# Background dots kept out of an FFN's first slice, and eight low parts per FFN taken from GpSimd to VectorE

## The chip, the cores and the metric

One core of one Trainium2 chip runs the whole program. The metric is device time in microseconds (us) of one execution. The engines are PE (TensorE matmul), PEld (TensorE's weight loads), DVE (VectorE), ACT (ScalarE), POOL (GpSimd) and SP (SyncE, which here issues the DMAs). L566 is line 566 of the kernel before.

## The reference, cut to what matters

A backbone of two layers. Each layer is an FFN, a token mixing, and a second FFN, so that there are four FFNs, which are called FFN 1 to FFN 4 here in the order of time. Tokens are 512 latent and 256 context columns (three groups of 256 columns, called G_A, G_B and G_C in the kernel, with G_C the context), the width is 1024, and the FFN's inner width is 2816. Everything is float32.

```python
def pre_mod(x, g, m, slot):
    return rmsnorm(x, g) * (1 + m[:, None, 3 * slot + 1]) + m[:, None, 3 * slot]

def post_residual(x, y, g, m, slot, weight):
    return x + weight * m[:, None, 3 * slot + 2] * rmsnorm(y, g)

def ffn_sublayer(x, m, slot, g_pre, g_post, wg, wu, wd):
    h = pre_mod(x, g_pre, m, slot)
    y = (jax.nn.silu(h @ wg) * (h @ wu)) @ wd
    return post_residual(x, y, g_post, m, slot, 0.5)
```

The vectors `m` (shift, scale and gate of each sub-layer) are a product of SiLU(c) with a matrix of 1024 x 9216 per layer. They depend on nothing else, so the kernel computes those of later sub-layers in the background, while matmuls run: these are the "dots" of this text.

## The kernel before, in words

**Products.** Every float32 operand is split into a high part (`whi`, `zh`, a rounded copy made by ACT) and a low part (`wlo`, `zl`, the remainder, a subtraction on DVE or POOL). A product is three matmuls: high by high, high by low, low by high (`mm3`, L519, L520, L522). Weights arrive as 128x1024 float32 tiles in a buffer with the tag "raw" (four of them), are copied by ACT to `whi` (L93) and subtracted to `wlo` (L94), on POOL unless the caller names DVE. `whi` and `wlo` have five buffers each.

**An FFN** (`ffn`) walks over 22 blocks `f` of 128 inner columns, in six slices of 4, 4, 4, 4, 2 and 4 blocks. In slice 0 the blocks 0 and 1, and the gate half of block 2 where there is no `begin`, are done group of tokens by group, since each group's input comes out of a chain of the norms before it (`post` and `prez`: squares on ACT, sums in the tiles `be` on DVE or POOL (L405), a matmul with ones on PE (L155), a power on POOL (L159), a broadcast by PE (L165), and the tiles of z from L469 on DVE). This first part of an FFN is called its head here. Block 2's other half follows, then block 3 and all later ones go through `fast`: seven products of half the width and half the depth, in the manner of Strassen, on sums and differences of the quarters. `combine` (L550 to L579) makes the combined inputs once per FFN, between the head and block 3: for each of four k the four DVE steps L560 to L563 on the tiles `y`, then a copy to `t42h` by ACT and the low part `t42l` on POOL (L566, 128x768; 128x512 in FFN 4, which has no context); at last for each k a copy of a half by ACT (L577) and its low part `t` on POOL (L578, 128x384; 128x256 in FFN 4). `combine_t1` (L581 to L586) adds four more pairs, with DVE. `evac` moves a block's result out of PSUM: SiLU by ACT (L546), the product `sg` on DVE (L547, at high priority), then `gh` on ACT and `gl` on DVE (L539). After each slice `down` multiplies by the down weights in chunks (two blocks of 128 rows of output each for a slice of four), first slice to `y` by ACT (L783), later slices added on DVE.

**Dots.** `ada_bg` (L353 on) puts items on the list `bg`: a load of a 128x1024 tile `abraw` into a "raw" buffer by SP (L237), and one or two dots on DVE (L243, one for each vector: two in the items before FFN 4's, one there). `pump` (L114 to L126) places them: each call adds `rate` to `credit`, with rate the items over 57; where no load is ahead it only issues one load and returns; otherwise it places items while the credit is at least 1, and each item also issues the next item's load. `pump(False)` adds credit alone. `ffn` calls it in block 2 after the gate half and after the evacuation, `fast` calls it twice per block (with `bg`, false for the last block of a slice), `down` once per chunk. The credit is carried from FFN to FFN.

**Order.** Each engine runs its queue in order. The order in a queue is that of a scheduler which plays the program on a simulated timeline: it takes program order as the priority among what is ready there, except for pieces under `high_priority`. So an instruction can stand in its engine's queue far from where the program places it.

The lines that the change touches: L566 and L578 in `combine`; L735 in the loop over a slice's blocks; and the three calls of `pump` in block 2 of slice 0 (L743, L751, L754).

Of the kernel before, what the change touches and what calls it, by code (L numbers as in the profile page):

```python
# [5 lines left out]
F32 = mybir.dt.float32  # L6
# [28 lines left out]
class K:  # L35
# [488 lines left out]
    def ffn(self, l, i, slot, groups, post, begin=None):  # L524

        nc, d = self.nc, self.d
# [5 lines left out]
        def loads(f, eng=None):  # L532
            return [self.load_w(d["wu"][l, i, f, u], eng=eng) for u in range(2)]
# [7 lines left out]
        def evac(j, pg, pu, off, n):  # L541
            for o in range(0, n, 256):
                sg = self.sg()[:, :256]
                c = slice(o, o + 256)
                with self.tc.high_priority():
                    nc.scalar.activation(sg, pg[:, c], AF.Silu)  # L546
                    nc.vector.tensor_tensor(out=sg, in0=pu[:, c], in1=sg, op=ALU.mult)  # L547
                gated(j, sg, off + o, 256)

        def combine():  # L550


            n1, n2, w = slice(0, nh), slice(nh, 2 * nh), 2 * nh
            t42 = [[self.tx(4 * x + k, f"t42{'hl'[x]}", F32R) for x in range(2)] for k in range(4)]
            t3 = [self.tx(8 + k, "t3", F32R) for k in range(4)]
            V = nc.vector
            F = {n: [] for n in ("b11", "b21", "b22", "t1", "t2", "t3", "t4")}
            for k in range(4):
                y0, y4 = self.y[k], self.y[k + 4]
                V.tensor_sub(y0[:, n1], y0[:, n2], y0[:, n1])  # L560
                V.tensor_sub(y0[:, n2], y4[:, n2], y0[:, n2])
                V.tensor_sub(y4[:, n2], y4[:, n2], y0[:, n1])
                V.tensor_sub(y4[:, n1], y4[:, n1], y4[:, n2])  # L563
                h, lo = t42[k]
                nc.scalar.copy(h[:, :w], y4[:, :w])
                nc.gpsimd.tensor_sub(lo[:, :w], y4[:, :w], h[:, :w].bitcast(F32))  # L566
                zh, zl = self.zh[k], self.zl[k]
                F["t3"].append((t3[k][:, :nh], t3[k][:, nh:w]))
                F["t4"].append((h[:, n1], lo[:, n1]))
                F["t2"].append((h[:, n2], lo[:, n2]))  # L570
                F["b11"].append((zh[:, n1], zl[:, n1]))
                F["t1"].append((zh[:, n2], zl[:, n2]))
                for n, c in (("b21", n1), ("b22", n2)):
                    F[n].append((self.zh[k + 4][:, c], self.zl[k + 4][:, c]))
            for k in range(4):
                th, tl = F["t3"][k]
                nc.scalar.copy(th, self.y[k][:, n2])  # L577
                nc.gpsimd.tensor_sub(tl, self.y[k][:, n2], th.bitcast(F32))  # L578
            return F  # L579

        def combine_t1(F):  # L581

            for k in range(4):
                h, lo = F["t1"][k]
                nc.scalar.copy(h, self.y[k][:, :nh])
                nc.vector.tensor_sub(lo, self.y[k][:, :nh], h.bitcast(F32))  # L586
# [69 lines left out]
        for s, nf in enumerate(SLICES):  # L656
            gh = [self.fp.tile([P, NT], F32R, tag=f"gh{j}", name=f"gh{j}") for j in range(nf)]
            gl = [self.fp.tile([P, NT], F32R, tag=f"gl{j}", name=f"gl{j}") for j in range(nf)]
            f0 = SL0[s]
            j0 = 0  # L660
            if s == 0:
                j0 = 2
                todo = groups
                W2 = None
                if begin is None:
                    W = [loads(f, nc.vector if (3 >> f) & 1 else None) for f in range(2)]
                    if 1:

                        W2 = self.load_w(d["wu"][l, i, 2, 0], eng=nc.vector if 0 else None)
                        pl, pc = self.bank(), self.bank() if has_c else None  # L670
                        part = {G_A: pl[:, 0:256], G_B: pl[:, 256:512], G_C: has_c and pc[:, :256]}
                else:

                    todo, W, pb = [G_C], [], {}

                    def part(f, ks):
                        for u in range(2):
                            wh, wl = W[f][u]
                            if (f, u) not in pb:
                                pb[f, u] = self.bank()  # L680
                            for k in ks:
                                self.mm3([(pb[f, u], 0, NL)], wh[:, k * P : (k + 1) * P], wl[:, k * P : (k + 1) * P], k, k == 0, k == KT - 1)

                    next(begin)
                    W.append(loads(0))
                    next(begin)
                    W.append(loads(1))
                    if 1:
                        next(begin)
                        part(0, range(4))  # L690
                        next(begin)
                        part(1, range(4))
                        for f in range(2):
                            part(f, (4, 5))
                    else:
                        part(0, range(4))
                        next(begin)
                        part(0, (4, 5))
                        part(1, range(6))
                        next(begin)  # L700
                    for f in range(2):
                        part(f, (6, 7))
                        evac(f, pb[f, 0], pb[f, 1], 0, NL)
                    next(begin)
                for g in todo:
                    off, n, v = g
                    self.drain(g)
                    for f in range(2):
                        ps = []
                        for u in range(2):  # L710
                            b = self.bank()[:, :n]
                            ps.append(b)
                            wh, wl = W[f][u]
                            for k in range(KT):
                                self.mm3([(b, off, n)], wh[:, k * P : (k + 1) * P], wl[:, k * P : (k + 1) * P], k, k == 0, k == KT - 1)
                                if k in ((3, 7) if 1 else (7,)):
                                    self.step()
                            if not 1:
                                self.step()
                        evac(f, ps[0], ps[1], off, n)  # L720
                    if W2:
                        wh, wl = W2
                        for k in range(KT):
                            self.mm3([(part[g], off, n)], wh[:, k * P : (k + 1) * P], wl[:, k * P : (k + 1) * P], k, k == 0, k == KT - 1)
                            if k == 3:
                                self.step()
                        self.step()
            if s == 0:
                self.drain()
                F = combine()  # L730
            for j in range(j0, nf):
                if f0 + j > 2:
                    if f0 + j == 3:
                        combine_t1(F)
                    fast(f0 + j, j, F, j < nf - 1)  # L735
                    continue
                ps = []
                pre = s == 0 and j == 2 and W2
                W = [None, self.load_w(d["wu"][l, i, 2, 1])] if pre else loads(f0 + j)
                for u in range(2):  # L740
                    if pre and u == 0:
                        ps.append([(pl, 0, NL)] + ([(pc[:, :256], NL, NC)] if has_c else []))
                        self.pump()  # L743
                        continue
                    wh, wl = W[u]
                    outs = [(self.bank()[:, :n], off, n) for off, n in full]
                    for k in range(KT):
                        self.mm3(outs, wh[:, k * P : (k + 1) * P], wl[:, k * P : (k + 1) * P], k, k == 0, k == KT - 1)
                    ps.append(outs)
                    if u == 0:  # L750
                        self.pump()  # L751
                for (pg, off, n), (pu, _, _) in zip(*ps):
                    evac(j, pg, pu, off, n)
                self.pump()  # L754
            self.down(d["wd"][l, i], SL0[s] * 1024, gh, gl, nf, s == 0, s == len(SLICES) - 1, groups, full, post, (l, slot))

    def down(self, wd, base, gh, gl, nf, first, last, groups, full, post, at):
# [1258 lines left out]
```

## Time and profile before

| | us |
|---|---|
| median of three runs | 3329.84 |
| lowest, highest run | 3324.64, 3330.06 |
| the profiled execution | 3321.82 |
| span of its profile | 3320.0 |
| FFN 2, FFN 3, FFN 4 in the span (about) | 1250 to 1790, 1793 to 2340, 2927 to 3320 |

Busy times are the time in which an engine executed instructions, as a share of the span. A wait of an engine is idle time in front of an instruction, put down to the instruction that released it (`PE rb L155 <- POOL be L405` is PE idle in front of a matmul of line 155 into `rb`, until POOL's operation of line 405 on `be` was done). The granted clock of PE is given as a share of its full speed of 2.4 GHz; its mean over this execution was 0.953. DVE steps that share memory with a POOL operation are longer than the same steps elsewhere, and the rows show it.

### The profile page before, as it was taken

The numbers are of one execution on the slowest core, as the hardware profiler recorded it, in microseconds if no ns is written. First come the engines' busy times: TensorE is split into PE (matmuls) and PEld (weight loads), VectorE is DVE, ScalarE is ACT, GpSimd is POOL, SyncE is SP. The second block draws the span as 40 slices with busy tenths as digits, with TensorE's granted clock in tenths as the row PEclk, the third lists the DMA queues.
The fourth block names the chain that finished last, engine by engine and source line by source line (L and its number), as shares of the span: only waits on it lengthen the run. The fifth ranks groups of instructions, "written<-read, shape, count | busy, mean of one in ns | idle before, by whom it ended". The sixth has DMA issues, their size and how long they took to land. (4 is left out here: it accounts for less than half of the span.)

```text
span 3320.0 us, 53695 instructions
## 1 busy us (share of the span) xinstructions
PE 3058.4 (92%) x20836; PEld 2785.7 (84%) x20836; DVE 2562.9 (77%) x4337; ACT 1377.4 (41%) x2600; POOL 1345.7 (41%) x1060
## 2 busy tenths in 40 slices
PE   7899999889889998999998899999989788989998
PEld 4799989878787798999998798999877676788998
DVE  7888887777778959677777977777677879776777
ACT  4333223544445644322234432223454346544343
POOL 5322122544655765222215511221544546753233
PEclk8999999889999899999999999999989899989999
DMA  6233333222310122323324233332322310224233
GB/s 221 101 122 122 107 127 117 94 73 54 97 64 10 51 86 81 108 91 107 101 73 158 82 109 114 121 127 89 104 98 64 88 46 17 91 90 134 96 106 98
DMA packets 149816, 318.68 MB, mean 96 GB/s; under 512 B 38185, under 2 KB 79529, under 8 KB 149561
## 3 DMA queue, kind: packets, MB, share of 16 engines
q1 hardware_dynamic: 149560, 315.25, 28.9%
q8 instruction: 163, 2.67, 0.3%
q14 instruction: 93, 0.75, 0.1%
HBM read 285.17 MB, written 30.03 MB: 95 GB/s over the span
## 5 line engine op out<-in xcount | busy, mean ns | idle before, releaser
L94 POOL TENSOR_TENSOR wlo<-wraw,whi 128x1024 fp32r<-128x1024 f32 (+1 forms) x228 | 580.3, 2554 | 1357.5 <-ACT whi L93 1304.9
L93 ACT CAST whi<-wraw 128x1024 fp32r<-128x1024 f32 (+2 forms) x482 | 469.5, 978 | 692.0 <-PE ps L776 338.5
L519 PE MATMUL ps<-zh,whi 128*128 128x256 f32 (+1 forms) x1208 | 389.5, 331 | 25.2 <-DVE sg L547 13.3
L608 PE MATMUL ps<-zh,whi 128*128 128x384 f32 (+1 forms) x1216 | 392.2, 323 | 8.0 <-DVE sg L547 4.5
L609 PE MATMUL ps<-zl,whi 128*128 128x384 f32 (+1 forms) x1216 | 392.1, 322 | 2.5 <-DVE zl L586 2.5
L610 PE MATMUL ps<-zh,wlo 128*128 128x384 f32 (+1 forms) x1216 | 390.8, 322 | 0.0
L520 PE MATMUL ps<-zl,whi 128*128 128x256 f32 (+1 forms) x1208 | 382.9, 327 | 5.0 <-DVE zl L477 5.0
L775 PE MATMUL ps<-gh,whi 128*128 128x512 f32 (+1 forms) x1008 | 349.5, 354 | 21.3 <-ACT gh L618 18.9
L776 PE MATMUL ps<-gl,whi 128*128 128x512 f32 (+1 forms) x1008 | 338.3, 352 | 17.3 <-DVE gl L619 17.3
L522 PE MATMUL ps<-zh,wlo 128*128 128x256 f32 (+1 forms) x1208 | 351.1, 324 | 0.0
L94 DVE TENSOR_TENSOR wlo<-wraw,whi 128x1024 fp32r<-128x1024 f32 (+1 forms) x254 | 298.1, 1175 | 31.3 <-ACT whi L93 29.9
L778 PE MATMUL ps<-gh,wlo 128*128 128x512 f32 (+1 forms) x1008 | 293.3, 348 | 0.0
L519 PEld LDWEIGHTS ps<-zh,whi 128*128 128x128 f32 x1208 | 236.8, 199 | 56.8 <-DVE sg L547 14.0
L520 PEld LDWEIGHTS ps<-zl,whi 128*128 128x128 f32 x1208 | 238.3, 198 | 24.5 <-DVE zl L477 6.1
L775 PEld LDWEIGHTS ps<-gh,whi 128*128 128x128 f32 x1008 | 191.7, 192 | 65.2 <-ACT gh L618 21.8
L608 PEld LDWEIGHTS ps<-zh,whi 128*128 128x128 f32 x1216 | 229.4, 189 | 10.9 <-ACT whi L93 4.8
L243 DVE CUSTOM_DVE_ANT_0 abraw<-abraw,srow 128x1024 f32<-128x1024 f32 x128 | 208.0, 1625 | 33.2 <-DMA abraw<-in_wat 31.2
L776 PEld LDWEIGHTS ps<-gl,whi 128*128 128x128 f32 x1008 | 193.5, 192 | 46.7 <-DVE gl L619 19.6
L609 PEld LDWEIGHTS ps<-zl,whi 128*128 128x128 f32 x1216 | 229.5, 189 | 3.5 <-DVE zl L586 3.2
L610 PEld LDWEIGHTS ps<-zh,wlo 128*128 128x128 f32 x1216 | 229.4, 189 | 0.0
L522 PEld LDWEIGHTS ps<-zh,wlo 128*128 128x128 f32 x1208 | 222.4, 199 | 6.5 <-issue 1.0
L243 DVE CUSTOM_DVE_ANT_0 adot<-abraw,srow 128x1024 bf16<-128x1024 f32 x96 | 151.3, 1576 | 63.2 <-DMA abraw<-in_wat 62.8
(394 smaller groups left out, 7722.3 us busy)
## 6 DMA issues: line engine op xcount, KB each, us to landing
wraw<-in_wu SPq DMA_DIRECT2D x176, 512.0 KB, 3.3
abraw<-in_wat SPq DMA_DIRECT2D x128, 512.0 KB, 3.3
wraw<-in_wd SPq DMA_DIRECT2D x88, 512.0 KB, 3.5
wraw<-in_wi SPq DMA_DIRECT2D x44, 512.0 KB, 3.4
wraw<-in_wo SPq DMA_DIRECT2D x16, 512.0 KB, 4.0
xs<-x SPq DMA_DIRECT2D x64, 128.0 KB, 1.7
x<-xs SPq DMA_DIRECT2D x64, 128.0 KB, 3.4
x<-in_x SPq DMA_DIRECT2D x48, 128.0 KB, 3.7
```

The source lines that it names most:

```text
L93: nc.scalar.copy(hi[:, :n], raw[:, :n])
L94: (eng or nc.gpsimd).tensor_sub(lo[:, :n], raw[:, :n], hi[:, :n].bitcast(F32))
L243: self.nc.vector.tensor_tensor_reduce(out=dst, in0=w, in1=self.srow[:, v, a:b], scale=1.0, scalar=start, op0=ALU.mult, op1=ALU.add, accum_ ...
L519: nc.tensor.matmul(ps, wh, self.zh[k][:, off : off + n], start=first, stop=False)
L520: nc.tensor.matmul(ps, wh, self.zl[k][:, off : off + n], start=False, stop=False)
L522: nc.tensor.matmul(ps, wl, self.zh[k][:, off : off + n], start=False, stop=last)
L608: nc.tensor.matmul(ps, w[0][:, c], xh, start=k == 0, stop=False)
L609: nc.tensor.matmul(ps, w[0][:, c], xl, start=False, stop=False)
L610: nc.tensor.matmul(ps, w[1][:, c], xh, start=False, stop=k == 3)
L775: nc.tensor.matmul(ps, wh[:, o : o + P], gh[j][:, off : off + n], start=j == 0, stop=False)
L776: nc.tensor.matmul(ps, wh[:, o : o + P], gl[j][:, off : off + n], start=False, stop=False)
L778: nc.tensor.matmul(ps, wl[:, o : o + P], gh[j][:, off : off + n], start=False, stop=j == nf - 1)
```

## The change

Eight subtractions per FFN in `combine` are issued to DVE instead of POOL (four at L566, four at L578). A flag `busy` is false in slice 0 of an FFN that has no `begin`, that is in FFN 2 to FFN 4; there the three pumps of block 2 add credit without placing anything, and so would those of `fast` in block 3, which had `False` already, as block 3 is the last of its slice. The pumps of `down` and of all later slices are as before. In FFN 1, which has `begin`, nothing changes in the pumps.

```diff
@@ combine
-                nc.gpsimd.tensor_sub(lo[:, :w], y4[:, :w], h[:, :w].bitcast(F32))
+                V.tensor_sub(lo[:, :w], y4[:, :w], h[:, :w].bitcast(F32))
...
-                nc.gpsimd.tensor_sub(tl, self.y[k][:, n2], th.bitcast(F32))
+                V.tensor_sub(tl, self.y[k][:, n2], th.bitcast(F32))
@@ ffn
+            busy = begin is not None or s > 0
...
-                    fast(f0 + j, j, F, j < nf - 1)
+                    fast(f0 + j, j, F, j < nf - 1 and busy)
...
-                        self.pump()
+                        self.pump(busy)
                         continue
...
                     if u == 0:
-                        self.pump()
+                        self.pump(busy)
                 for (pg, off, n), (pu, _, _) in zip(*ps):
                     evac(j, pg, pu, off, n)
-                self.pump()
+                self.pump(busy)
```

## Rows read from the trace of the kernel before

**Rows 1.** Busy time of each engine in us, its share of the span, instructions.

```profile
PE 3058.4 (92%) x20836; PEld 2785.7 (84%) x20836; DVE 2562.9 (77%) x4337; ACT 1377.4 (41%) x2600; POOL 1345.7 (41%) x1060
```

**Rows 2.** Waits of PE, whole span: us in total, times, longest.

```profile
PE rb L155 <- POOL be L405: 22.9, 8, 6.3
...
PE ps L519 <- DVE sg L547: 13.3, 3, 6.6
```

**Rows 3.** DVE's groups, 1796 to 1823: xcount, busy us, mean ns, idle before.

```profile
L243 DVE CUSTOM_DVE_ANT_0 adot<-abraw,srow 128x1024 bf16<-128x1024 f32 x4 | 6.9, 1732 | 0.0
L243 DVE CUSTOM_DVE_ANT_0 abraw<-abraw,srow 128x1024 f32<-128x1024 f32 x4 | 5.6, 1404 | 0.0
```

**Rows 4.** DVE's timeline, head of FFN 3: start, us, engine, line [idle before].

```profile
1795.35 1.26 DVE L469 SCALAR_TENSOR_TENSOR bt<-x,m,rb 128x256 f32<-128x256 f32 x3
...
1827.27 1.26 DVE L469 SCALAR_TENSOR_TENSOR bt<-x,m,rb 128x256 f32<-128x256 f32 x3 [1.24 <-PE rb L165]
```

**Rows 5.** PE's timeline in the same stretch.

```profile
1815.73 0.28 PE L522 MATMUL ps<-zh,wlo 128*128 128x256 f32 x1
1822.35 0.59 PE L155 MATMUL rb<-ones,be 128*128 128x1 f32 x2 [6.34 <-POOL be L405]
...
1844.13 0.38 PE L155 MATMUL rb<-ones,be 128*128 128x1 f32 x2 [1.52 <-POOL be L405]
```

**Rows 6.** Waits of PE, 1785 to 1850.

```profile
PE rb L155 <- POOL be L405: 7.9, 2, 6.3
```

**Rows 7.** One window: us, busy of PE, PEld, DVE, ACT, POOL, granted clock, DMA, GB/s.

```profile
1820.60:1830.60 10.00, 7.21 (x30) 6.74 (x31) 5.70 (x16) 4.37 (x12) 3.65 (x5) 0.50 0.09 31
```

**Rows 8.** Waits of PE, 2915 to 2965 (the head of FFN 4).

```profile
PE rb L155 <- DVE be L405: 4.9, 1, 4.9
PE rb L155 <- POOL be L405: 1.9, 1, 1.9
```

**Rows 9.** DVE's groups, 2927 to 2938.

```profile
L243 DVE CUSTOM_DVE_ANT_0 abraw<-abraw,srow 128x1024 f32<-128x1024 f32 x4 | 7.3, 1834 | 0.9 <-DMA abraw<-in_wat 0.9
```

**Rows 10.** Waits of PE, 1250 to 1300 (the head of FFN 2), the longest.

```profile
PE ps L519 <- ACT bt L404: 1.8, 1, 1.8
```

**Rows 11.** ACT's timeline, two chunks of `down` in FFN 2.

```profile
1364.47 0.86 ACT L783 COPY y<-ps 128x512 f32<-128x512 f32 x2 [5.70 <-PE ps L778]
...
1372.85 0.86 ACT L783 COPY y<-ps 128x512 f32<-128x512 f32 x2 [5.70 <-PE ps L778]
```

**Rows 12.** DVE's timeline, 1296 to 1316 (the combine of FFN 2).

```profile
1297.64 1.01 DVE L561 TENSOR_TENSOR y<-y,y 128x384 f32<-128x384 f32 x2
...
1308.69 4.77 DVE L563 TENSOR_TENSOR y<-y 128x384 f32<-128x384 f32 x2
1313.38 0.41 DVE L547 TENSOR_TENSOR sg<-ps,sg 128x256 f32<-128x256 f32 x1
```

**Rows 13.** One line's instructions: least, median, most ns, first and last start.

```profile
L586 DVE TENSOR_TENSOR zl<-y,zh x16: 412/546/555, 113.8 to 2988.3; 128x384 fp32r<-128x384 f32 x12, 128x256 fp32r<-128x256 f32 x4
```

**Rows 14.** POOL's groups, 1296.4 to 1313.4.

```profile
L94 POOL TENSOR_TENSOR wlo<-wraw,whi 128x1024 fp32r<-128x1024 f32 x2 | 5.4, 2676 | 0.0
L578 POOL TENSOR_TENSOR t<-y,t 128x384 fp32r<-128x384 f32 x4 | 5.0, 1282 | 1.1 <-ACT t L577 1.1
L566 POOL TENSOR_TENSOR t42l<-y,t42h 128x768 fp32r<-128x768 f32 x2 | 4.3, 2128 | 0.0
```

**Rows 15.** DVE's groups, 2000 to 2060 (in FFN 3's later blocks).

```profile
L94 DVE TENSOR_TENSOR wlo<-wraw,whi 128x1024 fp32r<-128x1024 f32 x5 | 6.1, 1220 | 0.0
L94 DVE TENSOR_TENSOR wlo<-wraw,whi 128x512 fp32r<-128x512 f32 x3 | 2.1, 693 | 0.0
```

**Rows 16.** Waits of PE, 105 to 150 (the combine of FFN 1).

```profile
PE ps L608 <- DVE sg L547: 2.4, 1, 2.4
```

**Rows 17.** Waits of PE, 2960 to 3000 (the combine of FFN 4).

```profile
PE ps L608 <- DVE sg L547: 2.1, 1, 2.1
```

**Rows 18.** DVE's timeline, 2977 to 2981 (FFN 4).

```profile
2978.53 0.42 DVE L547 TENSOR_TENSOR sg<-ps,sg 128x256 f32<-128x256 f32 x1 [1.58 <-ACT sg L546]
2980.50 1.73 DVE L94 TENSOR_TENSOR wlo<-wraw,whi 128x512 fp32r<-128x512 f32 x1 [1.55 <-ACT whi L93]
```

## The prediction

> **What bounds the kernel now.** Busy times first: PE is busy 92% of the span, DVE 77%, ACT and POOL 41% each [rows 1]. So a change to DVE's and POOL's work can only give back time in which PE waits, or runs at half clock after a wait. Next the waits of PE over the whole span, by releaser [rows 2]. Two groups concern this change. L155, the sums of a sandwich norm, waits 22.9 us for POOL's `be` adds, once for 6.3 us. L519 waits 13.3 us for `sg` of L547, a DVE eviction: two waits of 6.6 us and little else. I call the four FFNs FFN 1 to 4 in order of time. The 6.3 us lie at the head of FFN 3, the two of 6.6 us behind the combine of FFN 2 and of FFN 3.
>
> The profiled execution took 3321.82 us (span 3320.0); the median of the runs is 3329.84, 8.0 above. The sum below is made against the profiled execution and then taken off the median. About 0.2%, 6.7 us, is what a measurement of this kernel can tell from no change.
>
> **Part 1, the dots: what moves.** With `busy` false the three pumps of f=2 in slice 0 only add credit; the debt is worked off by the pumps behind the chunks of `down`. I followed credit and rate by hand. FFN 2: six dots (three items of two) leave f=2 and the first chunk's pump only issues one load; the second chunk's pump now places eight. FFN 3: eight leave f=2, and the second chunk's pump places fourteen. FFN 4 (one dot per item): three leave, and four come at once. FFN 1 has `begin` and keeps its order. No load or dot is added or dropped; `abraw` loads go to SP's queue later, past f=2's and f=3's weight loads.
>
> **Where those dots ran.** Not in f=2: DVE's order follows a schedule, and that had drawn most of them forward into the head of the FFN, where `post` and `prez` run on DVE. In FFN 3's head DVE runs eight dots between 1796 and 1823 us, 6.9 + 5.6 = 12.5 us [rows 3]. They lie in the chain of a norm. The first z operation of one token group is at 1795.35 and the next group's L155 at 1822.35, 27.0 us later; for the group after it, with no dots between, it is 1827.27 to 1844.13, 16.9 us [rows 4, 5]. PE's last product before the wait is at 1815.73 [rows 5]. Without dots L155 would be due at 1795.35 + 16.9 = 1812.3, before PE comes to it. So the 6.3 us [rows 6] close, with 0.6 of the small waits beside them: 6.9. Behind that gap the granted clock was 0.50, the 1.2 GHz level, for ten microseconds, with PE busy 7.21 [rows 7]: at 2.4 GHz half of that, 3.6, would be saved. Other waits of the head remain, so I take half, 1.8. FFN 3's head: 8.7 us, bounds 0 (the dots move back to other steps of the chain) and 10.5.
>
> FFN 4's head: L155 waits 4.9 and 1.9 us [rows 8] and DVE has four dots of 7.3 us there, one of them late for its load [rows 9]. POOL's adds end the smaller wait, so I take half of the 6.7: 3.4 (0 to 6.7). FFN 2's head: six dots, but no wait above 1.8 us, and that one for an ACT square [rows 10]: 0 (0 to 2.7, all its waits).
>
> **The burst.** A chunk of `down` lasts 8.4 us (1364.47 to 1372.85) [rows 11]; FFN 3's fourteen dots at 1.4 us (the lower mean of [rows 3]) are 20 us, more than two chunks. There are four raw buffers, and the third chunk's weight load is queued on SP behind seven `abraw` loads that wait for dots to free buffers. I take a loss of 3 us; bounds 0 (the schedule spreads the dots) and 20 (all of the dots in front of that load).
>
> **Part 2, the lows.** Eight subtractions per FFN go from POOL to DVE: four of 128x384 (`t`, L578) and four of 128x768 (`t42l`, L566), smaller in FFN 4. In FFN 2, DVE's combine runs from 1297.64 to 1313.38, 15.7 us for twelve steps and one small one [rows 12]. A 128x384 subtraction with two SBUF inputs takes 0.55 us where POOL is quiet [rows 13]: 12 × 0.55 + 0.4 = 7.0. Yet two L563 there take 4.8 [rows 12]: DVE's steps end with POOL's operation beside them. So 15.7 − 7.0 = 8.7 us are spent behind POOL, which in that time ran two `wlo` (5.4), four `t` (5.0) and one `t42l` (2.1; the second begins at 1313) [rows 14], 12.5 in all. The lows' share is 8.7 × 7.1 / 12.5 = 4.9. I charge DVE's wait in proportion to POOL's work.
>
> The Trainium skill, "SBUF — State Buffer", section "SBUF: two separate sides", says that DVE and GpSimd share one port pair under an exclusive lock held for the whole instruction, and that the loser fully blocks. By that rule the lows would return their whole 7.1 instead of 4.9, 2.2 more in FFN 2 and in FFN 3, and the sum would be 4.4 larger, near 3307. The stretched L563 agree with it; that DVE loses only 8.7 of 12.5 does not wholly.
>
> Three more `t42l` follow the eviction and cost DVE some 4.7 by the same share, so all lows return 9.6. On DVE they cost 4 × 0.55 + 4 × 0.95 = 6.0: 128x768 lies between 0.69 (128x512) and 1.22 (128x1024) [rows 15]. Net 3.6 us earlier per FFN. What counts is L547, for which PE waits. Of the lows between nothing and 4 × 0.55 + 2 × 0.95 = 4.1 can be queued ahead of it; I take 1.6, as the casts that they wait for come late. L547 is 4.9 − 1.6 = 3.3 earlier in FFN 2 and as much in FFN 3 (0 to 6.6, the whole wait, each). In FFN 1, where dots stay in the combine and the wait is 2.4 [rows 16], half of the net 3.6: 1.8. In FFN 4, half of a wait of 2.1 [rows 17]: 1.0. POOL's 6 to 13 us per FFN come free for `wlo`; nothing waits there, so 0.
>
> **Sum.** Heads 8.7 + 3.4 + 0 = 12.1; combine 1.8 + 3.3 + 3.3 + 1.0 = 9.4; burst −3. Together 18.5: 3303.3 against the profiled execution, 3311 against the median.
>
> **The rivals.**
> All closes: every wait named and the half-clock time go, heads 10.5 + 6.7 + 2.7 = 19.9, combine 6.6 + 6.6 + 3.6 + 2.1 = 18.9, no burst: 39, time 3291. For it: POOL leaves the whole combine stage. Against: `wlo` still share it. 0.13.
>
> The lows stand in front of L547: they cancel what POOL's absence gives, heads minus burst remain, 9 us, 3321. For it: program order puts them ahead. Against: evictions have high priority. 0.17.
>
> The dots do not set the head: POOL's adds end the longest wait [rows 6], and would be as late without dots. Combine minus burst remains, 6.4 us, 3323. Against: 27.0 beside 16.9 us [rows 4, 5]. 0.09.
>
> Slower: the lows wait on DVE for their ACT casts. In order, all behind them waits too: dots, evictions, `wlo`. DVE does wait like this for ACT, 1.58 us ahead of an L547 and 1.55 ahead of a `wlo` [rows 18]. Four `t42l` with 1.5 us each are 6 us per FFN, 24 in all; with the burst's 3 this is 27, less 12 for the heads, and the combine gains go: 15 above, 3345. It decides once L547 comes over 4 us later than now. Against: casts are short and ACT is 41% busy. 0.13.
> The Trainium skill, "TensorE: Matmul & The Clock Gate", section "Architectural detail: the array is 16× 32×32, not 1× 128×128", calls ACT's and DVE's queues strictly first-in-first-out. The two waits agree; if the casts came late, 3345 would follow.
>
> The change is not an empty one: sixteen instructions of each kind change engine.
>
> **How the numbers follow.** The forecast, 3311, has 0.48. Faster by over 0.2%: 0.46 of the forecast, all of "all closes", about half of "in front of L547" and a third of "dots do not set the head", 0.08 + 0.03: 0.70. Within 0.2%: the rest of these, 0.17. Slower: 0.13. The range, 3293 to 3333, leaves out half of "all closes" and most of the slower case, under 0.2; its upper end takes the burst at its bound of 20 with the forecast's gains, which is 3328, and some loss in the combine.
>
> **What would show it.** Right: no dot on DVE in the heads of FFN 2 to 4; FFN 3's L155 wait of 6.3 gone and the clock up behind it; no L566 or L578 on POOL; waits for `sg` of L547 about half of 13.3. Burst: seven `abraw` loads in a row in FFN 3's second chunk and a wait of L775 for `whi` or `gh` there. Wrong: DVE idle in front of lows with ACT as releaser, or a longer L547 wait; or the same wait at FFN 3's head without dots.

## The result, and the profile after

| | us |
|---|---|
| median before, four runs | 3329.46 |
| median after, four runs (3292.85 to 3299.77) | 3297.01 |
| ratio, 95% interval | 0.9905, 0.9887 to 0.9922 |
| profiled execution, before and after | 3321.82, 3296.14 |
| span, before and after | 3320.0, 3294.4 |

The change is faster by about 1%: 32.4 us between the medians, 25.7 us between the two profiled executions. The profiled execution of before was 7.6 us quicker than the median of its runs, that of after 0.9; the stages below add up to some 25 of the 25.7.

First the profile's busy times after the change.

```profile
PE 3056.4 (93%) x20836; PEld 2785.1 (85%) x20836; DVE 2550.1 (77%) x4369; ACT 1376.2 (42%) x2600; POOL 1298.7 (39%) x1028
```

Against [rows 1], DVE has 32 instructions more and yet 12.8 us less of busy time; POOL has 32 fewer and lost 47 us. The moved work costs DVE less than the stretching that went with it: with the lows alone (experiment 1) DVE's busy time is 2547.8 us, 15.1 less, and with the gate alone (experiment 2) 2563.9, 1.0 more.

Next the waits of PE after the change, whole span.

```profile
PE ps L778 <- DVE gl L619: 25.4, 11, 3.6
PE ps L777 <- ACT gh L618: 16.7, 9, 4.0
...
PE rb L155 <- POOL be L405: 15.8, 7, 3.8
```

The same two waits for `gl` and `gh` before (L776 and L775 of before are L778 and L777 now):

```profile
PE ps L775 <- ACT gh L618: 18.9, 8, 4.0
PE ps L776 <- DVE gl L619: 17.3, 8, 3.5
```

Against [rows 2], no wait for `sg` of L547 is left, and L155's longest wait for POOL is down from 6.3 to 3.8. What grew is the wait for `gl`, one of the two results of a `fast` block on their way to `down`, from 17.3 to 25.4 us; that for `gh`, the other one, fell from 18.9 to 16.7.

Where the time went is seen by setting the same matmul of both traces side by side. The table gives, for FFN 2 and FFN 3, the time from the first matmul of one stage to the first of the next, in us, read off PE's records. "Block 2's end" begins with the up half of block 2 and contains the combine; "down 0" is the down product of slice 0. All columns but "before" and "change" are experiments told below.

| | before | lows only | gate only | change | lows, gated down | both, gated down |
|---|---|---|---|---|---|---|
| FFN 2 head | 49.0 | 49.0 | 47.4 | 45.9 | 49.1 | 45.9 |
| FFN 2 block 2's end | 17.5 | 9.3 | 16.1 | 8.4 | 8.9 | 8.4 |
| FFN 2 block 3 | 16.2 | 20.8 | 14.8 | 18.7 | 15.9 | 15.3 |
| FFN 2 down 0 | 33.5 | 39.8 | 42.8 | 39.5 | 33.5 | 35.6 |
| FFN 3 head | 67.3 | 66.9 | 57.0 | 57.5 | 68.3 | 58.0 |
| FFN 3 block 2's end | 17.2 | 9.7 | 16.8 | 8.4 | 8.4 | 8.4 |
| FFN 3 block 3 | 16.6 | 20.7 | 14.9 | 20.9 | 14.9 | 15.4 |
| FFN 3 down 0 | 39.2 | 40.9 | 38.9 | 40.6 | 37.1 | 33.5 |
| FFN 3 slice 1's blocks | 58.3 | 58.3 | 63.2 | 58.3 | 58.3 | 65.7 |

Taken this way the change wins 3.1 us in the head of FFN 2, 9.8 in that of FFN 3 and 1.5 in that of FFN 4, some 9 us in the stage of the combine in each of FFN 2 and FFN 3, and 8.9 in FFN 1 (its block 3, where the combine's waits lay, goes from 23.8 to 14.9; 2.5 of that is given back in the down products of slices 1 and 2). Then it loses 8.5 us in block 3 and down 0 of FFN 2 and 5.7 in those of FFN 3. FFN 4's head has more than these 1.5 us, since its waits of L155 stand mostly in front of its first matmul: from the last matmul of the token mixing to that first one the change gains 3.8 us (waits of 4.9 and 1.9 us before, 2.7 and 0.9 after), after it had lost 2.7 between FFN 3's slices and the end of the mixing, for a reason that is open. As a measure of what such a stage varies by: with the gate alone, which leaves FFN 1 as it was, FFN 1's block 3 takes 24.7 us for 23.8.

**The combine of FFN 2 after the change.** DVE's timeline, and POOL's below it.

```profile
1290.84 1.02 DVE L562 TENSOR_TENSOR y<-y,y 128x384 f32<-128x384 f32 x2
...
1292.25 0.55 DVE L578 TENSOR_TENSOR t<-y,t 128x384 fp32r<-128x384 f32 x1
...
1296.46 0.42 DVE L547 TENSOR_TENSOR sg<-ps,sg 128x256 f32<-128x256 f32 x1
1296.80 2.44 DVE L563 TENSOR_TENSOR y<-y 128x384 f32<-128x384 f32 x1
1299.16 3.16 DVE L566 TENSOR_TENSOR t42l<-y,t42h 128x768 fp32r<-128x768 f32 x1
```

```profile
1293.90 4.92 POOL L94 TENSOR_TENSOR wlo<-wraw,whi 128x1024 fp32r<-128x1024 f32 x1 [3.40 <-PE ps L522]
```

L547 starts 7.9 us after the combine's first L561 (1288.56); before it was 15.7 [rows 12]. Of the steps between, only one is longer than 0.55 us (an L561 of 1.09, beside a POOL operation of line 477), and four lows of 0.55 are among them. POOL's `wlo` shows 4.92 us where [rows 14] have 2.7: so this time, as I read it, it is POOL that was held, behind DVE's steps in a row, and it ends 2.4 us after DVE came to L547. Only then do DVE's L563 and L566 stretch, and L547 is past.

**The head of FFN 3 after the change.** Waits of PE, 1780 to 1845, and a window of it (columns as in [rows 7]).

```profile
PE ps L519 <- ACT zh L472: 2.0, 2, 1.1
PE rb L155 <- DVE be L405: 1.3, 2, 0.9
```

```profile
1802.00:1814.00 12.00, 10.73 (x62) 10.08 (x62) 8.20 (x21) 8.05 (x21) 6.01 (x9) 0.72 0.04 12
```

The wait of 6.3 us [rows 6] is gone, and no dot is left on DVE in this stretch. Some half clock stays: 0.72 in the mean of these 12 us, where [rows 7] had 0.50 over ten.

**Block 3 of FFN 2 after the change.** Waits of PE from the block's first matmul to slice 1, then DVE's timeline at the longest, then the matmul that waited.

```profile
PE ps L778 <- DVE gl L619: 3.6, 1, 3.6
PE ps L608 <- ACT whi L93: 2.2, 1, 2.2
```

```profile
1332.06 2.57 DVE L243 CUSTOM_DVE_ANT_0 abraw<-abraw,srow 128x1024 f32<-128x1024 f32 x1
...
1334.56 1.22 DVE L243 CUSTOM_DVE_ANT_0 adot<-abraw,srow 128x1024 bf16<-128x1024 f32 x1
...
1335.71 0.56 DVE L617 TENSOR_TENSOR ps<-ps,p 128x384 f32<-128x384 f32 x1
1336.18 0.54 DVE L619 TENSOR_TENSOR gl<-ps,gh 128x384 fp32r<-128x384 f32 x1
```

```profile
1336.77 0.39 PE L778 MATMUL ps<-gl,whi 128*128 128x256 f32 x1 [3.56 <-DVE gl L619]
```

The dots that left block 2 stand here, two of them between L617 and L617: 3.8 us of dots in front of the `gl` for which PE waits 3.56. Program order has them behind the second chunk of down 0; DVE's order has drawn them forward to between the evictions of block 3.

### The profile page after: what moved, and what is told of

The parts are those of the page before. It is cut to its first block, busy times and chain, and to the rows that moved or that the text cites. A ratio compares the mean times of both kernels' runs of the same rounds, so it can differ in the third digit from the quotient of the medians.

```text
span 3294.4 us, 53696 instructions
## 1 busy us (share of the span) xinstructions
PE 3056.4 (93%) x20836; PEld 2785.1 (85%) x20836; DVE 2550.1 (77%) x4369; ACT 1376.2 (42%) x2600; POOL 1298.7 (39%) x1028
## 5 line engine op out<-in xcount | busy, mean ns | idle before, releaser
L94 POOL TENSOR_TENSOR wlo<-wraw,whi 128x1024 fp32r<-128x1024 f32 (+1 forms) x228 | 589.6, 2596 | 1396.5 <-ACT whi L93 1357.5
L777 PE MATMUL ps<-gh,whi 128*128 128x512 f32 (+1 forms) x1008 | 350.6, 356 | 17.7 <-ACT gh L618 16.7
L778 PE MATMUL ps<-gl,whi 128*128 128x512 f32 (+1 forms) x1008 | 341.4, 354 | 25.4 <-DVE gl L619 25.4
L519 PEld LDWEIGHTS ps<-zh,whi 128*128 128x128 f32 x1208 | 234.5, 198 | 38.5 <-ACT zh L472 11.2
L777 PEld LDWEIGHTS ps<-gh,whi 128*128 128x128 f32 x1008 | 193.4, 194 | 61.8 <-ACT gh L618 19.5
L778 PEld LDWEIGHTS ps<-gl,whi 128*128 128x128 f32 x1008 | 194.6, 193 | 54.9 <-DVE gl L619 27.9
L608 PE MATMUL ps<-t42h,whi 128*128 128x384 f32 (+1 forms) x608 | 197.3, 324 | 7.6 <-ACT whi L93 7.6
```

Source lines behind the costliest of these rows:

```text
L94: (eng or nc.gpsimd).tensor_sub(lo[:, :n], raw[:, :n], hi[:, :n].bitcast(F32))
L519: nc.tensor.matmul(ps, wh, self.zh[k][:, off : off + n], start=first, stop=False)
L608: nc.tensor.matmul(ps, w[0][:, c], xh, start=k == 0, stop=False)
L777: nc.tensor.matmul(ps, wh[:, o : o + P], gh[j][:, off : off + n], start=j == 0, stop=False)
L778: nc.tensor.matmul(ps, wh[:, o : o + P], gl[j][:, off : off + n], start=False, stop=False)
```

## The experiments

The experiments ran in three series: 1 to 4; 5, 6, 10 and 11; and 7, 8, 9 and 12. Each series had its own runs of the kernel before (medians 3327.23, 3326.75 and 3329.93 in this order), and the ratios stand to these.

**1. The lows alone.**

```diff
-            busy = begin is not None or s > 0
+            busy = True
```

> The changed kernel with busy always true: the eight low parts per FFN on VectorE, the dots placed as before. Theory (the stages' own times, as matched instructions of the two traces show them: FFN 1's combine about 6.5 us earlier, FFN 2's 5, FFN 3's 8, FFN 4's 2, in sum some 21): if the lows do this alone, about 3309 us, with the two 6.6 us waits of L519 for sg gone, the 6.3 us wait at FFN 3's head still there, and no loss in block 3 of slice 0. The prediction's sizes: 9.4 us, 3320. Rival (the lows pay only where the dots are out of the way, since both stand in VectorE's queue): under 6.7 us, 3323 or more.

Measured: 3320.62 us, ratio 0.9977 (0.9968 to 0.9986): 6.6 us between the medians. The prediction had 9.4; its 3320 is met only because the kernel before was quicker in this series. The gain is the rival's (under 6.7 us), though the time is not (3323 or more). Yet the first step of the theory holds: FFN 2's and FFN 3's block 2's end are 8.2 and 7.5 us shorter (table). What fails is "no loss in block 3", and the rival's reason, dots in the way in VectorE's queue, is borne out by experiment 5. Windows from FFN 2's block 3 to slice 1, before and here, and the waits of PE and two rows of DVE here:

```profile
1324.10:1373.80 49.70, 48.33 (x278) 43.81 (x277) 30.81 (x48) 18.96 (x33) 12.95 (x5) 1.00 0.40 137
```

```profile
1310.50:1371.10 60.60, 52.68 (x279) 46.51 (x278) 37.70 (x57) 19.22 (x33) 12.91 (x5) 0.94 0.34 113
```

```profile
PE ps L608 <- ACT whi L93: 4.0, 2, 3.4
PE ps L778 <- DVE gl L619: 1.9, 1, 1.9
PE ps L777 <- DVE p L633: 1.9, 1, 1.9
```

```profile
1330.13 3.38 DVE L243 CUSTOM_DVE_ANT_0 adot<-abraw,srow 128x1024 bf16<-128x1024 f32 x1 [3.27 <-DMA abraw<-in_wat]
...
1333.44 0.54 DVE L633 TENSOR_TENSOR p<-p,ps 128x384 f32<-128x384 f32 x1
```

Before, this stretch took 49.7 us at full clock; now 60.6, with 7.9 us in which PE stands still and a clock of 0.94. One of the waits is plain in DVE's rows: a dot waits 3.27 us for its own load, is then stretched, and the eviction L633 stands behind it.

**2. The gate alone.** Both subtractions are back on POOL; the rest is the change.

> The changed kernel with the low parts back on GpSimd: only the dots moved. Theory (matched instructions: heads of FFN 2, 3 and 4 earlier by about 6, 11 and 4.5 us, and a loss of about 9 and 5.5 us in block 3 and the first chunks of slice 0 in FFN 2 and FFN 3): net 5 to 9 us faster, 3321 to 3325, with the 6.3 us wait at FFN 3's head gone and the 6.6 us waits of L519 for sg still there. The prediction's sizes: 12.1 less 3, 3320. Rival (the debt of dots in block 3 takes back all): 3330 or more.

Measured: 3316.36 us, ratio 0.9966 (0.9953 to 0.9978), 10.9 us, more than theory and prediction had. The wait at FFN 3's head is gone and the waits for L547 stay, 5.0 us in FFN 2 and 5.7 in FFN 3, as the theory had it. FFN 2's block 3 and down 0 lose 7.9 us:

```profile
1316.90:1374.50 57.60, 51.22 (x278) 45.12 (x277) 40.38 (x60) 18.85 (x33) 14.86 (x5) 0.94 0.44 145
```

```profile
PE ps L777 <- ACT gh L618: 4.9, 1, 4.9
```

The two parts by themselves make 17.5 us; together they make 32.4. By the table, FFN 2 (its four rows added) costs 116.2 us before, 118.9 with the lows alone, 121.1 with the gate alone and 112.5 with both. There each part alone loses 8 to 11 us in block 3 and down 0, and both together lose 8.5: the same loss, paid once. This makes 11.3 of the 15 us that the two parts have together beyond their sum. FFN 3 has 3.0 more of it, and less plainly: its five rows are 198.6 us before, 196.5 with the lows alone, 190.8 with the gate alone and 185.7 with both. There the gate alone loses nothing against before in block 3 and down 0 (53.8 for 55.8 us), but 4.9 us in slice 1's blocks.

**3. No debt of dots in down 0.** The changed kernel, and the pumps of slice 0's `down` only add credit too.

```diff
+            busy = self.busy = begin is not None or s > 0
...
-                if 1: self.pump()
+                self.pump(self.busy)
```

> The changed kernel, but the pumps behind the chunks of slice 0's down in FFN 2 to 4 also only add credit, so that the debt is placed from slice 1 on. Its dots no longer stand between the evictions of block 3 in VectorE's queue, but behind them. Theory (the loss of the changed kernel is the dots in front of block 3's evictions, for which PE waits 3.6 us for gl in FFN 2 and 2.2 in FFN 3, at half clock beside it): 10 to 15 us faster than the change, 3282 to 3287. Rival (the loss is the debt itself, wherever it lies, since its loads hold raw buffers that weights need): the same as the change, 3297, or slower, with waits of PE for whi in slice 1.

Measured: 3284.86 us, ratio 0.9871 (0.9857 to 0.9884). The theory's number; the rival falls, though part of the debt is paid later: FFN 3's slice 1 takes 65.7 us for 58.3 (table). The window from block 3 to slice 1 in FFN 2 is back to full clock:

```profile
1308.10:1359.00 50.90, 48.71 (x279) 43.90 (x278) 43.71 (x68) 18.40 (x33) 12.85 (x5) 1.00 0.48 157
```

**4. The gate in FFN 1 too** (`busy = s > 0`).

> The changed kernel with busy false in FFN 1's slice 0 too. Theory (FFN 1's gain came from the lows, its combine has 4.7 us of waits left, and the dots that leave its head come back in block 3): within 3 us of the change, 3294 to 3300. Rival (FFN 1's head has the same trouble as those of FFN 3): 6 to 10 us faster than the change, 3287 to 3291.

Measured: 3298.54 us, ratio 0.9914 (0.9900 to 0.9928): the theory's range, no gain. The dots that leave its block 2 come back: nine stand between the evictions of block 3, where the change has five, and down 0 takes 46.4 us for 40.8 before. Waits of PE from 105 to 180 us:

```profile
PE ps L777 <- ACT gh L618: 5.1, 1, 5.1
PE ps L778 <- DVE gl L619: 2.4, 1, 2.4
```

**5. The lows, with block 2's dots as before and none from down 0.** Experiment 3 with plain `self.pump()` in block 2.

> The low parts on VectorE, the dots of block 2 placed as before, but the pumps behind the chunks of slice 0's down in FFN 2 to 4 only add credit: no dots come from there into block 3. Theory (the lows alone lost their gain of about 8 us each in FFN 2 and FFN 3 to dots that stand between block 3's evictions in VectorE's queue, 10.9 and 5.7 us): that loss comes back, 3306 to 3312. Rival (PE's lead is lost to weights that arrive no earlier, whatever the dots do): 3317 to 3322, as with the lows alone.

Measured: 3294.68 us, ratio 0.9906 (0.9891 to 0.9921): 32 us, far more than the theory's 15 to 21. The rival falls: weights did not hold PE back. FFN 2's block 3 to slice 1:

```profile
1306.50:1355.90 49.40, 48.61 (x278) 43.74 (x277) 31.92 (x56) 18.68 (x33) 12.27 (x5) 1.00 0.42 139
```

```profile
PE ps L610 <- DVE wlo L94: 0.7, 1, 0.7
```

60.6 us with the dots of down 0 in block 3, 49.4 without: this is what the lows lost. They need not have the gate of block 2 to get it back. A count shows the same. Between block 3's first eviction and its last `gl` in FFN 2, DVE runs two dots before (3.2 us), three with the lows alone (7.8 us, and 4.1 us of waiting for their loads), seven with the gate alone (10.5), ten with the change (17.0), and one in experiments 3, 5 and 6. The count by itself doesn't give the loss: in FFN 3 the gate alone has ten dots there (13.9 us) for four before (7.1), and loses no more than before.

**6. The same edit of down 0 in the kernel before.**

> The kernel before, with nothing changed but that the pumps behind the chunks of slice 0's down in FFN 2 to 4 only add credit. Theory (dots in block 3 cost the kernel before next to nothing, since PE came to block 3 late, after its 6.6 us wait, and they ran in that time): within 4 us of before, 3323 to 3329. Rival (they cost 10 us or more by themselves, and the change has nothing to do with it): 3312 to 3318.

Measured: 3316.28 us, ratio 0.9969 (0.9958 to 0.9981), 10.5 us. The rival is right here, and my theory, that the dots of down 0 cost nothing before, falls. By the stages it is 1.6 us in FFN 2 and 7.7 in FFN 3 (block 3 14.6, down 0 33.5). But 10.5 for this edit and 6.6 for the lows make 17, and both together make 32. With down 0's dots out of the way on both sides, the lows are worth 21.6 us (3316.28 to 3294.68, one series); with them in place, 6.6. My reading is that what dots between evictions cost depends on how early PE arrives; no run shows that by itself.

**7. The larger lows back on POOL, and 8. the smaller ones.** Each is the change with one of the two lines undone.

> The changed kernel with the four larger low parts (t42l, 128x768) back on GpSimd and the four of 128x384 (t) on VectorE. Theory (the wait for L547 comes from GpSimd's operations in front of it, and of the lows these are the four t and one t42l): L519's wait for sg falls from 6.6 to 2 us or less, combine of FFN 2 and FFN 3 keeps 6 to 8 of its 9 us, 3299 to 3305. Rival (by GpSimd time, as the prediction charged it: t is 5.0 of 13.5 us of lows): under half is kept, 3308 to 3314.

> The changed kernel with the four smaller low parts (t, 128x384) back on GpSimd and the four of 128x768 (t42l) on VectorE. Theory (VectorE's steps alternate with GpSimd's t, four of 1.3 us beside steps of 0.5): L519's wait for sg stays at 3 to 5 us in FFN 2 and FFN 3, 3303 to 3310. Rival (the larger ones are what holds VectorE, being 8.5 of 13.5 us of lows): the wait is under 2 us, 3297 to 3302.

Measured: 3314.36 us, ratio 0.9952 (0.9937 to 0.9967), with the 128x384 ones on DVE; 3301.12 us, ratio 0.9912 (0.9895 to 0.9928), with the 128x768 ones. The waits for L547 came as the theories had them, the times nearer to the rivals'. With the small ones on DVE, L547 causes no wait in FFN 2 or 3 and block 2's end keeps its 9 us, but the next wait of PE is longer. Waits of PE in FFN 2 from there to slice 1, then DVE's rows and POOL's:

```profile
PE ps L608 <- ACT whi L93: 6.1, 1, 6.1
PE ps L777 <- ACT gh L618: 4.6, 1, 4.6
```

```profile
1305.81 1.73 DVE L539 TENSOR_TENSOR gl<-sg,gh 128x256 fp32r<-128x256 f32 x1
1307.46 2.34 DVE L596 TENSOR_TENSOR wraw<-wraw 128x512 f32<-128x512 f32 x1
1309.73 2.86 DVE L243 CUSTOM_DVE_ANT_0 adot<-abraw,srow 128x1024 bf16<-128x1024 f32 x1
```

```profile
1304.95 9.30 POOL L566 TENSOR_TENSOR t42l<-y,t42h 128x768 fp32r<-128x768 f32 x4
```

Beside the four `t42l` DVE's steps behind L547 are stretched, among them L596 (2.34 us for 0.68 after the change), and L597 to L599, which with it make block 3's weight sums, start only behind them; so `whi` comes late. With the larger ones on DVE, POOL's `t` and DVE's steps alternate. Waits of PE in FFN 2 from the combine on, DVE's rows and POOL's:

```profile
PE ps L519 <- DVE sg L547: 4.3, 1, 4.3
PE ps L778 <- DVE gl L619: 3.4, 1, 3.4
```

```profile
1294.66 2.67 DVE L562 TENSOR_TENSOR y<-y,y 128x384 f32<-128x384 f32 x2
```

```profile
1294.29 3.91 POOL L578 TENSOR_TENSOR t<-y,t 128x384 fp32r<-128x384 f32 x3
```

So the part that removes the wait for L547 is worth 4.7 us over the gate alone by the ratios (0.9966 to 0.9952, times 3327), which by the intervals can't be told from nothing, and the other one 18, though the wait for L547 stays.

**9. POOL's weight subtractions in the combine, alone.** The kernel before, with block 2's second `wlo` and block 3's first on DVE.

```diff
-            w0 = self.cut(wg)
+            w0 = self.cut(wg, eng=V if f == 3 else None)
...
-                W = [None, self.load_w(d["wu"][l, i, 2, 1])] if pre else loads(f0 + j)
+                W = [None, self.load_w(d["wu"][l, i, 2, 1], eng=nc.vector)] if pre else loads(f0 + j)
```

> The kernel before with one edit: the two low parts of weights (128x1024) that GpSimd subtracts in the combine stage are on VectorE; lows of the combine and dots as before. Theory (any operation of GpSimd holds VectorE's steps, whoever wants its result: 2 x 2.7 us less, 2 x 1.2 more, and less for the lows to fall on): L519's wait for sg falls from 6.6 to 2 to 4 us in FFN 2 and FFN 3, and block 3 gives most of it back as with the lows alone, 3318 to 3325. Rival (only the lows hold it): the wait stays above 5 us, 3325 to 3330.

Measured: 3321.74 us, ratio 0.9975 (0.9965 to 0.9985). The time fits the theory and the waits don't. In FFN 2 PE waits as long as before, now for `wlo`, and in FFN 3 5.8 us for `sg` of L547; this is FFN 2, from block 2's end to slice 1:

```profile
PE ps L522 <- DVE wlo L94: 5.9, 1, 5.9
PE ps L776 <- DVE gl L619: 1.5, 1, 1.5
```

The stages of the combine gain 0.4 and 0.5 us: without the lows' removal the weights' does next to nothing there. Of the 8 us between the medians the two profiled executions show 4.1, and about as much lies in FFN 3's block 3 and down 0 (51.8 for 55.8 us); where the rest is stays open.

**10 to 12. Beyond the change.** Experiment 3 with experiment 9's edit; experiment 3 with at most two items per pump; both.

```diff
         ran = False
+        left = 2
-        while self.credit >= 1 and self.bg:
+        while self.credit >= 1 and self.bg and left:
+            left -= 1
```

> The kernel with gated down pumps, and the two low parts of weights (128x1024) that GpSimd still subtracts in the combine stage also on VectorE: block 2's second half and block 3's first. Theory (VectorE's steps are held while GpSimd's subtraction runs: 2.4 and 3.2 us for steps of 0.5 and 0.9 beside them, while one on VectorE takes 1.2): combine ends 1 to 3 us earlier, and since PE hardly waits there any more, 3281 to 3287. Rival (VectorE becomes the bound in block 3, and the weights come later): 3290 or more.

> The kernel with gated down pumps, and at most two items placed by any pump, so that FFN 3's debt of nineteen dots is worked off over several pumps. Theory (that burst costs the stretch from slice 1's first block to its down some 7 us in FFN 3): 3277 to 3281. Rival (VectorE's order takes the dots forward to the same places, or the loss only moves to slice 1's end): 3283 to 3288.

> The change with gated down pumps, at most two items per pump, and the two low parts of weights in the combine stage on VectorE. Theory (the two last steps touch other stretches, slice 1 of FFN 3 and the combine): both gains add, 3275 to 3279. Rival (both leads end in the same wait for block 3's evictions): 3280 to 3284, as each alone.

Measured: 3280.39 us, ratio 0.9861 (0.9845 to 0.9876); 3280.79, ratio 0.9861 (0.9848 to 0.9875); 3274.70, ratio 0.9837 (0.9823 to 0.9852). All within a microsecond of the theories' ranges; the last is the fastest of this study, 55 us below before and 22 below the change (of another series). The intervals don't tell either step alone from experiment 3; but neither interval of a single step holds the ratio of both, though the intervals overlap. So both together are faster than each alone, as far as this tells. By the stages the places are not those of the theories. With the weights' low parts on DVE, FFN 2 gains 0.5 us in the combine with block 3 and 2.1 in down 0. With the cap, FFN 3's slice 1 has its blocks in 58.9 us for 65.7, but the down product behind them takes 45.1 for 39.7: most of the loss moves to the end of slice 1, as the rival had it. These are the waits of PE in slice 1 and its `down` without the cap (from 1930 us), then with it, in the blocks (from 1890 us) and in the `down` (from 1953 us; its lines stand two further down).

```profile
PE ps L608 <- DVE gl L619: 2.9, 2, 1.8
PE ps L778 <- DVE gl L619: 2.3, 1, 2.3
```

```profile
PE ps L610 <- DVE gl L621: 0.3, 1, 0.3
```

```profile
PE ps L779 <- ACT gh L620: 4.3, 1, 4.3
PE ps L780 <- DVE gl L621: 4.1, 1, 4.1
```

## Why the prediction was right, and where its terms were not

The measured time lies in the range and the sign was right. The sum of 18.5 us was made against the profiled execution, where the change is worth 25.7. The single terms missed by more than their sum: the combine was worth 16 us more than I had, the burst cost 11 more, and that these largely cancelled is luck.

**FFN 3's head: 8.7, measured 9.8.** The dots were in the chain of the norm. The gate alone shortens this head by 10.3 us, the lows alone by 0.4. The rival by which POOL's adds set the wait falls.

**The other heads: 3.4 for FFN 4 and 0 for FFN 2, measured 1.5 and 3.1 from their first matmul on.** In FFN 4 the 3.8 us in front of that matmul belong to the head too, though 2.7 had been lost ahead of it. L155 still waits there, 2.7 us for DVE and 2.0 for POOL, where it had 4.9 and 1.9. In FFN 2 two waits of L155 close, 0.9 and 0.7 us; the rest of the 3.1 is mostly six matmuls of L155 that now run in front of the first matmul, where the change loses 0.5. So the head gains 2.7, the whole of the upper bound. The granted clock is 1.00 in this head before and after, the 2.4 GHz level, so no half clock is in it.

**The combine: 3.3 each in FFN 2 and FFN 3, 1.8 in FFN 1 and 1.0 in FFN 4; measured 9.1, 8.8, 8.9 (6.4 after what slices 1 and 2 give back) and 0.7.** The step that failed is "I charge DVE's wait in proportion to POOL's work". Taking the lows off POOL gave back nearly all of the 8.7 us that DVE spent behind POOL in front of L547, the share of `wlo` included: the one `wlo` that now starts in front of L547 stretches no step of DVE there, and the other comes behind it. The Trainium skill's "SBUF — State Buffer", section "SBUF: two separate sides", whose rule I set beside the term, gave 5.5 (7.1 less 1.6) as I applied it and was nearer, and still too small: I priced the lows alone with it, and not that the `wlo` would then be out of the way. That either engine can be the one that waits, as the rule has it, the 4.92 us `wlo` shows. Experiments 7 and 8 correct the prediction in another point: I valued only L547, and the lows behind it are worth more in time. For FFN 1 I took half because dots stay in the combine; the experiment with the lows alone shows 8.0 there with the dots in place. One figure of the sum is off by itself: the three other `t42l` are 4.4 us at the 2.13 us of [rows 14], not 4.7, which takes 0.3 from the net of 3.6.

**The burst: −3 in FFN 3, measured −8.5 in FFN 2 and −5.7 in FFN 3.** The step that failed is the place. I put the debt where the program places it, behind the second chunk, and charged a weight load behind `abraw` loads. I had found that DVE's order draws dots forward into the head, and did not apply it to the debt: it was drawn forward into block 3, in front of the evictions. The sign that I gave for it, a wait in FFN 3's down 0 for `whi` or `gh`, shows 1.8 us for `gh` and none for `whi`. Experiment 3 removes the burst from down 0 and gives 11 to 12 us (ratio 0.9871 after 0.9905). One reading of the program was wrong beside it: in FFN 2 to FFN 4 two of the three pumps of block 2 run, since L751 is reached only where the gate half is not done in the head.

**That the two parts add.** My sum took this for granted, and alone they gave 6.6 and 10.9, close to the terms that I had (9.4, and 12.1 less 3). The 15 us on top are for the most part the loss in FFN 2's block 3 and down 0, that each part brings by itself and that the change pays once. For the lows this is shown by experiment 5 against 1; for the gate I take it from the windows of experiment 2 and did not run the gate with the gated `down` and the lows on POOL. That each part's own median came near to its term is no proof of the terms: both had a larger gain and a loss that I had not seen.

**The slower rival.** No low waited for its cast in front of L547 in FFN 2: they stand there at 0.47 us from each other. That everything closes, 3291, was nearer to the measured time than the forecast by 8 us, but not by its mechanism: the gaps closed, and new ones opened in block 3.

## What to carry to other kernels

Look where an instruction stands in its engine's queue, not where the program places it: a background operation that is "behind" a stage may stand in front of that stage's evictions, and can then cost nearly its whole length (3.6 us of PE's wait behind 3.8 us of dots). The price of an operation beside which another engine's steps stretch is not its share of the stretching; taken away, it can move the others out of the critical stretch too. And when two parts end in the same later wait, measure them together and apart, since each alone may show much less than it is worth: the lows showed 6.6 us alone and 21.6 with the dots of down 0 out of the way.

## What I had not expected of the hardware

A POOL subtraction that started out of idle while DVE had two-input steps in a row took 4.92 us instead of 2.7, and ended 2.4 us after DVE's first step that reads PSUM; experiments 1, 3 and 7 show the same (4.6 to 4.9 us). In the combine of FFN 2 before [rows 12, 14], where POOL's operations mostly followed each other without a pause, DVE and POOL took turns one by one, and a `t` that started out of idle there, with DVE's steps in a row too, was not held:

```profile
1304.55 1.14 POOL L578 TENSOR_TENSOR t<-y,t 128x384 fp32r<-128x384 f32 x1 [1.10 <-ACT t L577]
```

Which of the two orders comes when is left open. And a wait cost more than its own length: experiment 1's stretch from FFN 2's block 3 to slice 1 has 7.1 us more of PE standing still than experiment 5's (7.9 for 0.8) and is 11.2 us longer. With 6 to 8 us in which PE stood still in FFN 2's block 3 and down 0 the mean granted clock was 0.94 over 58 to 61 us (experiments 1 and 2 and the change), with 0.8 to 2.2 us it was 1.00 over 49 to 51 us (before and experiments 3 and 5).
